# Attention values as the stationary operand, two key groups in column halves, and a division whose row sums travel through DRAM

## The chip, the cores and the metric

One core of a Trainium2 chip runs the whole program: two stacks of transformer blocks on 256 tokens of width 1024, in one launch, all in fp32. The metric is the device time of one execution in microseconds. TensorE multiplies, VectorE and ScalarE do the elementwise work, GpSimd (POOL) is nearly unused, and SP issues the DMAs.

## The reference

The first stack has two layers of feed-forward, mixer, feed-forward; so has the second, with another mixer. What the change touches is the attention in each mixer and the matmul that takes its output:

```python
def windowed_gqa(q, k, v, sink):                 # first stack: 8 heads, 2 key groups of 4 heads, head size 64
    scores = einsum('bnqhgd,bnkhd->bhgnqk', qb, kb) * (HEAD_DIM ** -0.5)
    scores = where(valid, scores, -1e30)
    probs = softmax(concatenate([scores, sink_logit], -1), -1)[..., :-1]
    out = einsum('bhgnqk,bnkhd->bnqhgd', probs, vb)
...
y_attn = windowed_gqa(q, k, v, attn_sink) @ w_br_attn
...
def swa_sink_attention(q, k, v, sinks, band_bias, band_mask):   # second stack: 16 heads, 2 key groups of 8 heads
    m = maximum(max(s, -1, keepdims=True), sink)
    e = exp(s - m)
    p = e / (sum(e, -1, keepdims=True) + exp(sink - m))
    o = einsum('bnkgqs,bnskd->bnqkgd', p, vb)
...
branch = einsum('blmc,mcd->blmd', ys, w_branch[l])    # ys[2] is the attention's output
```

## The kernel before, in words

A token block is 128 tokens (t = 0, 1) and lies on the 128 partitions. Every large matmul (`mm`, lines 346 to 361) takes its activations transposed, as pairs of a rounded part `ah` and a rest `al`, and its weights as pairs `whi` and `wlo`; three products L359, L360, L361 replace one exact fp32 product. A weight unit is two blocks of 128 rows by 512 columns: SP loads it into `raw` (`load_raw`, L253), ScalarE rounds it to `whi` (L268), VectorE takes the rest `wlo` (L274). For a unit TensorE does 12 products: two row blocks, two token blocks, three products each. The splits run several units ahead (`ahead`: 7 in the first mixer, 6 in the second), and up to four raw units wait besides.

The order of all engines is the order of the code. After each unit a `tick` (L319 on) issues the splits, then delayed pieces of work (`later`), then one step of the first task in a list. The attentions are such tasks: `attend1` (L639, first mixer) runs beside the gate projections, `attend2` (L852, second mixer) beside the three convolution projections and the gates of branch 2. In the first mixer the branch matmul that takes `yatt` follows right behind the task, in the second it is `branch(2, yatt, ...)`.

Both attentions go through `pipeline` (L700) in units u: a unit is a token block and four or eight heads. In iteration u it issues scores(u) and values(u - 2), then, one tick later, exps(u) and turn(u - 1).

- scores: fp32 products of head size 64 on half of the array's rows, even and odd heads in turn (L663, L875); VectorE adds the band or the bias and takes the row maxima (L580).
- exps: ScalarE's exponentials with row sums `den` (L588).
- turn: TensorE transposes the exponentials (L473), VectorE and ScalarE copy them to `pT` (L679, L681, L895, L897).
- values (L683, L899): for every head and key block a product with `pT` as the stationary operand, 128 by 128, and 64 columns of v moving (L690, L908). The output has queries on partitions. When eight heads are there, `inv_den` (L591) computes the reciprocals of the row sums, VectorE multiplies the PSUM tile by them, broadcast along the free axis (L695, L915), and in the next iteration `put_T` (L476) transposes the result with four TensorE transposes (L473) and splits it into `ah` and `al` (L485 on ScalarE, L487 on VectorE). These are the activations `yatt` of the branch matmul.

Small PSUM tiles come from four rotating buffers (`sm`), SBUF tiles of 2 KB per partition from twelve (`half`), and those of 4 KB from 41 (`big`).

Of the kernel before, what the change touches and what calls it, by code (L numbers as in the profile page):

```python
# [21 lines left out]
P = 128  # L22
# [111 lines left out]
def units(name, idx, segs, nkt):  # L134
    return [(name, idx, k, min(2, nkt - k), tuple(segs)) for k in range(0, nkt, 2)]
# [63 lines left out]
class Net:  # L199
# [53 lines left out]
    def load_raw(self):  # L253
        name, idx, k, m, segs = self.plan[self.raw_at]
# [221 lines left out]
    def put_T(self, act, kt0, t, src, m, scale=None, col=None, later=None):  # L476
# [6 lines left out]
        if col is None:  # L483
            o, l_ = hi[:, j0:j0 + m, ts], lo[:, j0:j0 + m, ts]
            nc.scalar.activation(o, ps[:, :m], AF.Copy, scale=1.0 if scale is None else scale)  # L485
            if scale is None:
                nc.vector.tensor_tensor(l_, ps[:, :m], o.bitcast(F32), ALU.subtract)  # L487
            else:
                nc.vector.scalar_tensor_tensor(l_, ps[:, :m], scale, o.bitcast(F32), ALU.mult, ALU.subtract)
        else:  # L490
            for j in range(m):
                nc.scalar.activation(hi[:, j0 + j, ts], ps[:, j], AF.Copy, scale=col(kt0 + j))  # L492
            for j in range(m):
# [3 lines left out]
                low() if later is None else later.append(low)  # L497

# [92 lines left out]
    def inv_den(self, den, mx, sink, n):  # L591

        nc = self.nc
        e = self.tiny([P, n])
# [3 lines left out]
        r = self.tiny([P, n])  # L598
        nc.vector.reciprocal(r, e)
        return r  # L600

# [37 lines left out]
    def attend1(self, l, qk, v, yatt):  # L639
# [11 lines left out]
        mx, den, po, sc, pT = {}, {}, {}, {}, {}  # L651
# [20 lines left out]

        def turn(u):
            s = sc.pop(u)
            p = pT[u] = self.big([P, 2, 4, P], s="pT")
            for kb in range(2):
                ps = self.transposed([s[:, h, kb * P:(kb + 1) * P] for h in range(4)])
                if kb:
                    nc.scalar.activation(p[:, kb], ps, AF.Copy)  # L679
                else:  # L680
                    nc.vector.tensor_copy(p[:, kb], ps)  # L681
# [16 lines left out]
        yield from self.pipeline(4, scores, exps, turn, values)  # L698

    def pipeline(self, n, scores, exps, turn, values):  # L700

        last = None
        for u in range(n + 2):
            if last is not None:
                last()
                last = None
            if u < n:
                scores(u)
            if u >= 2:
                last = values(u - 2)  # L710
# [6 lines left out]
        if last is not None:  # L717
            last()
# [25 lines left out]
    def mixer1(self, l, prep, nxt, after=None):  # L744
# [43 lines left out]
        for m, (gen, act, wb) in enumerate(((pool, ypool, "w_branch_pool"), (att, yatt, "w_branch_attn"))):  # L788
# [6 lines left out]
            for h in range(2):  # L795
                self.branch(act, units(wb, (l,), [(h * 512, 512, 0)], 4), th[h], y, h, m == 0)
# [55 lines left out]
    def attend2(self, l, qT, kd, va, yatt):  # L852
# [9 lines left out]
        plan = [(0, 0, 8), (0, 8, 8), (1, 0, 4), (1, 4, 4), (1, 8, 4), (1, 12, 4)]  # L862
        mx, den, po, sc, pT = {}, {}, {}, {}, {}
# [22 lines left out]

        def turn(u):
# [3 lines left out]
            blocks = [(e, kb) for e in range(per) for kb in range(t + 1)]  # L891
# [7 lines left out]
        def values(u):  # L899
            t, h0, per = plan[u]  # L900
            kv = h0 // 8
            if h0 % 8 == 0:
# [537 lines left out]
```

## Time and profile before

| | before |
|---|---|
| median of 3 runs | 2532.87 us (2532.43 to 2534.51) |
| the profiled execution | 2532.06 us |
| its span, first to last instruction | 2530.3 us |
| granted TensorE clock | 0.999 of 2.4 GHz |
| busy: TensorE, VectorE, ScalarE, GpSimd | 99%, 63%, 49%, 0% |

The sum in the prediction is made against the profiled execution; the runs stand some 0.8 us above it. In the rows, `sm<-v,pT` names the output tile and what it was computed from, PEld is a weight load, and a line number is a line of the kernel before. An fp32 product outside the large matmuls appears as two records.

### The profile page before, as it was taken

Reading aid. Unit: us, or ns where it says so; the run is one execution under the profiler, and the core shown is the slowest. Engines: PE = TensorE matmul, PEld = TensorE weight load, DVE = VectorE, ACT = ScalarE, POOL = GpSimd, SP = SyncE. Lnnn points to the kernel's source line nnn. Section 1 sums busy time; section 2 is a strip of 40 time slices with the busy share of each in tenths; the row PEclk is TensorE's granted clock in tenths of the full one; section 3 lists DMA queues with packets and bytes.
Section 4 is the critical chain, followed back from the end, with each engine's and each line's share of the span. In section 5 each row is a group of like instructions: output and inputs, shape, how many; then the busy total and the mean of one; then the engine's idle time right before and its main releaser. Section 6 shows DMA issues by size and latency. Waiting matters only on the chain.

```text
span 2530.3 us, 31764 instructions
## 1 busy us (share of the span) xinstructions
PE 2516.7 (99%) x12017; PEld 2083.6 (82%) x12017; DVE 1584.5 (63%) x2592; ACT 1239.3 (49%) x1882; POOL 0.2 (0%) x4
## 2 busy tenths in 40 slices
PE   9999999999999999999999999999999999999998
PEld 7888888888888888888888888888888888888887
DVE  6545665555546755655697777755654788776653
ACT  5435554444445544444474545543543664544542
POOL 0000000000000000000000000000000000000000
PEclk9999999999999999999999999999999999999999
DMA  8666555655564655655644566655656644566652
GB/s 285 212 203 211 158 191 166 201 188 174 178 218 149 199 167 186 200 178 187 207 125 142 175 192 196 199 175 194 197 168 199 184 130 146 185 194 206 185 179 79
DMA packets 252790, 462.26 MB, mean 183 GB/s; under 512 B 17707, under 2 KB 43996, under 8 KB 252508
## 3 DMA queue, kind: packets, MB, share of 16 engines
q1 hardware_dynamic: 252636, 460.23, 57.9%
q8 instruction: 94, 1.54, 0.2%
q14 instruction: 60, 0.49, 0.1%
HBM read 459.10 MB, written 4.22 MB: 183 GB/s over the span
## 4 chain that ended last, share of the span: by engine, by line
PE 95%; DVE 2%; ACT 2%; DMA 0%; issue 0%; SPq 0%; DVEq 0%; ACTq 0%
PE mm L359 29%; PE mm L361 29%; PE mm L360 29%; PE sm L473 4%; PE sm L908 1%; PE sm L690 1%; PE sm L1073 1%; DVE wlo L274 0%; ACT sc L588 0%; DVE acc L975 0%; PE sm L663 0%; ACT acc L968 0%; PE sm L1140 0%; ACT whi L268 0%; DVE sc L580 0%
## 5 line engine op out<-in xcount | busy, mean ns | idle before, releaser
L359 PE MATMUL mm<-whi,ah 128*128 128x512 f32 x3360 | 1326.2, 395 | 0.6 <-ACT whi L268 0.6
L361 PE MATMUL mm<-whi,al 128*128 128x512 f32 x3360 | 1304.5, 388 | 0.0
L360 PE MATMUL mm<-wlo,ah 128*128 128x512 f32 x3360 | 1301.9, 387 | 0.8 <-DVE wlo L274 0.8
L274 DVE TENSOR_TENSOR wlo<-raw,whi 128x1024 fp32r<-128x1024 f32 (+2 forms) x840 | 976.3, 1210 | 106.1 <-ACT whi L268 102.3
L268 ACT ACTIVATE whi<-raw 128x1024 fp32r<-128x1024 f32 (+2 forms) x840 | 829.2, 1048 | 104.8 <-PE mm L360 58.2
L361 PEld LDWEIGHTS mm<-whi,al 128*128 128x128 f32 x3360 | 630.7, 188 | 133.9 <-DVE al L495 4.1
L359 PEld LDWEIGHTS mm<-whi,ah 128*128 128x128 f32 x3360 | 631.3, 188 | 127.1 <-issue 4.3
L360 PEld LDWEIGHTS mm<-wlo,ah 128*128 128x128 f32 x3360 | 631.7, 188 | 126.3 <-issue 1.9
L485 ACT ACTIVATE ah<-sm 128x512 fp32r<-128x512 f32 (+1 forms) x124 | 64.7, 568 | 468.9 <-PE sm L473 465.5
L487 DVE TENSOR_TENSOR al<-sm,ah 128x512 fp32r<-128x512 f32 (+1 forms) x108 | 65.9, 647 | 170.7 <-ACT ah L485 170.7
L512 DVE SCALAR_TENSOR_TENSOR hid<-mm,s,silu 128x512 f32<-128x512 f32 (+1 forms) x96 | 66.9, 705 | 167.8 <-PE mm L361 153.8
L492 ACT ACTIVATE ah<-sm,cols 128x128 fp32r<-128x128 f32 x240 | 67.6, 374 | 146.8 <-PE sm L473 140.2
L495 DVE SCALAR_TENSOR_TENSOR al<-sm,cols,ah 128x128 fp32r<-128x128 f32 x240 | 68.1, 345 | 68.5 <-ACT ah L492 68.5
L507 ACT ACTIVATE silu<-mm,s 128x512 f32<-128x512 f32 (+1 forms) x96 | 62.0, 655 | 91.6 <-PE mm L361 90.7
L560 DVE SCALAR_TENSOR_TENSOR yg<-mm,post 128x512 f32<-128x512 f32 x24 | 16.6, 692 | 121.0 <-ACT sq L461 121.0
L544 DVE SCALAR_TENSOR_TENSOR x<-mm,x 128x512 f32<-128x512 f32 x24 | 16.5, 689 | 110.8 <-PE mm L361 110.8
L461 ACT ACTIVATE sq<-mm 128x512 bf16<-128x512 f32 x24 | 14.3, 597 | 125.8 <-PE mm L361 125.8
L613 ACT ACTIVATE gate<-gate 128x512 f32<-128x512 f32 x40 | 25.1, 632 | 52.1 <-DVE gate L612 51.7
L473 PEld LDWEIGHTS sm<-c_ident,hid 128*128 128x128 f32 x352 | 41.2, 140 | 6.8 <-DVE hid L512 0.7
L473 PE MATMUL sm<-c_ident,hid 128*128 128x128 f32 x352 | 46.5, 272 | 0.1
L588 ACT ACTIVATE sc<-sc,s 128x256 f32<-128x256 f32 (+1 forms) x96 | 43.9, 459 | 3.7 <-DVE s L583 3.6
L461 ACT ACTIVATE sq<-x 128x1024 bf16<-128x1024 f32 x26 | 27.4, 1069 | 22.6 <-DVE x L544 17.5
(200 smaller groups left out, 1022.0 us busy)
## 6 DMA issues: line engine op xcount, KB each, us to landing
raw<-in_ffn_w SPq DMA_DIRECT2D x248, 512.0 KB, 4.2
raw<-in_w_in SPq DMA_DIRECT2D x200, 512.0 KB, 3.7
raw<-in_w_ffn_in SPq DMA_DIRECT2D x160, 512.0 KB, 3.8
raw<-in_w_ffn_out SPq DMA_DIRECT2D x88, 512.0 KB, 3.9
raw<-in_w_branch SPq DMA_DIRECT2D x48, 512.0 KB, 3.5
raw<-in_w_out SPq DMA_DIRECT2D x32, 512.0 KB, 3.7
raw<-in_ffn_w SPq DMA_DIRECT2D x32, 256.0 KB, 3.0
raw<-in_w_ffn_in SPq DMA_DIRECT2D x32, 256.0 KB, 3.2
```

Source lines behind the costliest of these rows:

```text
L268: self.nc.scalar.activation(hi[:, :m, :width], raw[:, :m, :width], AF.Copy)
L274: self.nc.vector.tensor_tensor(lo[:, :m, :width], raw[:, :m, :width], hi[:, :m, :width].bitcast(F32), ALU.subtract)
L359: nc.tensor.matmul(ps[:, :n], a_h, hi[:, j, :n], start=(kt == 0), stop=False)
L360: nc.tensor.matmul(ps[:, :n], a_h, lo[:, j, :n], start=False, stop=False)
L361: nc.tensor.matmul(ps[:, :n], a_l, hi[:, j, :n], start=False, stop=(kt == nkt - 1))
L473: self.nc.tensor.transpose(ps[:, j, :], a, self.ident)
L485: nc.scalar.activation(o, ps[:, :m], AF.Copy, scale=1.0 if scale is None else scale)
L487: nc.vector.tensor_tensor(l_, ps[:, :m], o.bitcast(F32), ALU.subtract)
L492: nc.scalar.activation(hi[:, j0 + j, ts], ps[:, j], AF.Copy, scale=col(kt0 + j))
L495: nc.vector.scalar_tensor_tensor(lo[:, j0 + j, ts], ps[:, j], col(kt0 + j), hi[:, j0 + j, ts].bitcast(F32), ALU.mult, ALU.subtract)
L507: nc.scalar.activation(s[:, :n], ps, AF.Silu, scale=prep.rstd[t])
L512: nc.vector.scalar_tensor_tensor(h[:, :n], ps, prep.rstd[t], s[:, :n], ALU.mult, ALU.mult)
```

## The change

The roles in the value product are swapped. For a block of four heads e of each key group g, v of the group (128 keys by 64) is stationary and the transposed exponentials of the four heads (128 keys by 512) move. The group g writes to partitions 64g to 64g + 63 of one PSUM tile, in a column half of the array: group 0 in columns 0 to 63, group 1 in columns 64 to 127. The output is already transposed, channels on partitions, so the four transposes fall away. The reciprocal of a row sum now has to lie along the free axis and be the same on 64 partitions: POOL writes the reciprocals to a DRAM tile `rd` and reads them back, spread over 64 partitions for each group, to `rden`. `norm` does this one iteration after the scores; the multiply (`rest`) comes at the start of the iteration after the values. A unit's values need both groups: half of the units issue none, the others one block of four products (the first token block of `attend2` two blocks of two). `attend2` takes its units in another order for this.

The channels now lie in another order on the partitions: the first 64 hold heads of group 0, the others of group 1. The branch weights are loaded to match, each half of the partitions by a DMA of its own (`groups=2`).

```diff
-def units(name, idx, segs, nkt):
-    return [(name, idx, k, min(2, nkt - k), tuple(segs)) for k in range(0, nkt, 2)]
+def units(name, idx, segs, nkt, groups=1):
+
+    return [(name, idx, k, min(2, nkt - k), tuple(segs), groups) for k in range(0, nkt, 2)]
...
-            self.nc.sync.dma_start(raw[:, :m, at:at + n],
-                                   w[k * P:(k + m) * P, c0:c0 + n].rearrange("(k p) n -> p k n", p=P))
+            rows = w.shape[0] // groups
+            d = P // groups
+            for g in range(groups):
+                r = g * (rows if groups > 1 else 0)
+                self.nc.sync.dma_start(raw[g * d:(g + 1) * d, :m, at:at + n],
+                                       w[r + k * d:r + (k + m) * d, c0:c0 + n].rearrange("(k p) n -> p k n", p=d))
...
+    def spread(self, r, ne):
+
+        d = self.dp.tile([2, ne, P], F32, name=self.name("rd"))
+        self.nc.gpsimd.dma_start(d.rearrange("g e q -> q g e"), r)
+        out = []
+        for e in range(0, ne, 4):
+            R = self.half([P, 4, P], s="rden")
+            for g in range(2):
+                self.nc.gpsimd.dma_start(R[g * 64:g * 64 + 64].rearrange("p e q -> p (e q)"),
+                                         d[g, e:e + 4].rearrange("e q -> (e q)").partition_broadcast(64))
+            out.append(R)
+        return out
+
+    def weighted(self, v, pT, nkb, R, yatt, kt0, t):
+
+
+        nc = self.nc
+        ps = self.smp([P, 4, P])
+        for kb in range(nkb):
+            for g in range(2):
+                nc.tensor.matmul(ps[g * 64:g * 64 + 64].rearrange("p e q -> p (e q)"), v[kb][:, g * 64:g * 64 + 64],
+                                 pT[g][:, 4 * kb:4 * kb + 4].rearrange("p e q -> p (e q)"),
+                                 start=(kb == 0), stop=(kb == nkb - 1))
+
+        def rest():
+            o = self.half([P, 4, P], s="att")
+            nc.vector.tensor_tensor(o, ps, R, ALU.mult)
+            self.put(yatt, kt0, t, o, 4)
+        return rest
...
+        def norm(u):
+            t, half = divmod(u, 2)
+            if half == 1:
+                r[t] = self.spread(self.inv_den(den[t], mx[t], sink, 0, 4), 4)
...
         def values(u):
             t, half = divmod(u, 2)
-            if half == 0:
-                po[t] = self.smp([P, 8, 64])
-            p = pT.pop(u)
-            for e in range(4):
-                for kb in range(2):
-                    nc.tensor.matmul(po[t][:, half * 4 + e], p[:, kb, e], v[kb][:, half * 64:half * 64 + 64],
-                                     start=(kb == 0), stop=(kb == 1))
             if half == 1:
-                r = self.inv_den(den[t], mx[t], sink, 8)
-                o = self.half([P, 8, 64], s="att")
-                nc.vector.tensor_tensor(o, po[t], bcast(r, 2, 64), ALU.mult)
-                return lambda: self.put_T(yatt, 0, t, o.rearrange("p h d -> p (h d)"), 4)
+                return [self.weighted(v, [pT.pop(u - 1), pT.pop(u)], 2, r.pop(t)[0], yatt, 0, t)]
...
-        for u in range(n + 2):
-            if last is not None:
-                last()
-                last = None
+        for u in range(n + 3):
+            for f in rest or ():
+                f()
+            rest = ()
             if u < n:
                 scores(u)
-            if u >= 2:
-                last = values(u - 2)
+            if 1 <= u <= n:
+                norm(u - 1)
+            if 2 <= u < n + 2:
+                rest = values(u - 2)
+            if u == n + 2:
+                return
             yield
...
-        plan = [(0, 0, 8), (0, 8, 8), (1, 0, 4), (1, 4, 4), (1, 8, 4), (1, 12, 4)]
+        plan = [(0, 0, 8), (0, 8, 8), (1, 0, 4), (1, 8, 4), (1, 4, 4), (1, 12, 4)]
...
+            if h0 >= 8:
+                r[u] = self.spread(self.inv_den(den[t], mx[t], sinks, h0 - 8, per), per)
...
+            return [self.weighted(va, [q[:, e0:] for q in p] if t == 0 else p, t + 1, d[e0 // 4], yatt, h0 - 8 + e0, t)
+                    for e0 in range(0, per, 4)]
```

`put` is the second half of `put_T` without the transposes: ScalarE's rounding copy and VectorE's subtraction.

The change rewrites the order of several engines. Three places of it follow, as listings of the program, one line an instruction.

TensorE in the first attention, layer 0, before: the end of one weight unit, the transposes of the first token block's output (`att`), a block of eight value products, and the first product of the next unit.

```order
L361 MATMUL mm_2337<-whi_2216,al_1607 128x512
L473 MATMUL sm_2472<-c_ident,att_2417 128x128 x4
L690 MATMUL sm_2479<-v_1853,pT_2441 128x64
L690 MATMUL sm_2479<-v_1864,pT_2441 128x64
L690 MATMUL sm_2479<-v_1853,pT_2441 128x64
L690 MATMUL sm_2479<-v_1864,pT_2441 128x64
L690 MATMUL sm_2479<-v_1853,pT_2441 128x64
L690 MATMUL sm_2479<-v_1864,pT_2441 128x64
L690 MATMUL sm_2479<-v_1853,pT_2441 128x64
L690 MATMUL sm_2479<-v_1864,pT_2441 128x64
L359 MATMUL mm_2496<-whi_2238,ah_1604 128x512
```

The same engine in the change, at the last value block of this attention, between two weight units:

```order
L366 MATMUL mm_2491<-whi_2273,al_1605 128x512
L636 MATMUL sm_2541<-pT_2436,v_1853 64x512
L636 MATMUL sm_2541<-pT_2510,v_1853 64x512
L636 MATMUL sm_2541<-pT_2436,v_1864 64x512
L636 MATMUL sm_2541<-pT_2510,v_1864 64x512
L364 MATMUL mm_2490<-whi_2309,ah_1606 128x512
```

Two key groups (`pT_2436`, `pT_2510`) alternate, 64 output partitions each; four products stand where 16 of 64 columns stood in two blocks, and no transposes follow.

VectorE in the second attention, layer 0, before: the reciprocals of the row sums of eight heads, the multiply of the PSUM tile, the next weight split.

```order
L595 TENSOR_TENSOR s_10841<-rows,s_10514 128x8
L597 TENSOR_TENSOR s_10841<-s_10841,s_10515 128x8
L599 RECIPROCAL s_10845<-s_10841 128x8
L915 TENSOR_TENSOR att_10847<-sm_10832,s_10845 128x512
L274 TENSOR_TENSOR wlo_10861<-raw_10644,whi_10805 128x1024
```

In the change the chain ends with the reciprocals of all sixteen heads of token block 0, and a weight split follows at once, with no multiply behind it:

```order
L596 TENSOR_SCALAR s_10657<-s_10657 128x4
L609 TENSOR_TENSOR s_10671<-rows,s_10474 128x16
L611 TENSOR_TENSOR s_10671<-s_10671,s_10475 128x16
L613 RECIPROCAL s_10675<-s_10671 128x16
L279 TENSOR_TENSOR wlo_10705<-raw_10518,whi_10651 128x1024
L1025 SCALAR_TENSOR_TENSOR acc_10501<-th_10653,acc_10501 128x512
```

Thirty rows later comes the multiply, between a weight split and the row maxima of the next scores; it takes the spread tile `rden`:

```order
L279 TENSOR_TENSOR wlo_10841<-raw_10649,whi_10804 128x1024
L642 TENSOR_TENSOR att_10852<-sm_10782,rden_10679 128x512
L508 TENSOR_TENSOR al_10346<-att_10852,ah_10345 128x4x128
L642 TENSOR_TENSOR att_10856<-sm_10785,rden_10682 128x512
L508 TENSOR_TENSOR al_10348<-att_10856,ah_10347 128x4x128
L593 ISA sc_10860,s_10657<-sm_10861,T_9997,rows 128x256
```

POOL in the change, where the first stack's last attention ends and the second's begins: the write of the reciprocals `s` of eight heads to DRAM, element by element, and two reads back; then the write of sixteen heads and four reads; then eight again. Before, POOL has no DMA at all.

```order
L619 DMA rd_6610<-s_6608 128x8x1
L624 DMA rden_6612<-rd_6610 64x512 x2
L619 DMA rd_10677<-s_10675 128x16x1
L624 DMA rden_10679<-rd_10677 64x512 x2
L624 DMA rden_10682<-rd_10677 64x512 x2
L619 DMA rd_10878<-s_10876 128x8x1
```

Each write is followed at once by its reads, which can start only when it has landed. The program has ten writes and 24 reads.

## Rows read from the trace of the kernel before

**Rows 1.** The page's first part: busy time, share and instructions of each engine.

```profile
PE 2516.7 (99%) x12017; PEld 2083.6 (82%) x12017; DVE 1584.5 (63%) x2592; ACT 1239.3 (49%) x1882; POOL 0.2 (0%) x4
```

**Rows 2.** The page's chain that ended last, by engine.

```profile
PE 95%; DVE 2%; ACT 2%; DMA 0%; issue 0%; SPq 0%; DVEq 0%; ACTq 0%
```

**Rows 3.** Groups of TensorE by line and shape: xcount | busy us, mean ns.

```profile
L908 PE MATMUL sm<-va,pT 128*128 128x64 f32 x192 | 23.6, 276 | 1.0 <-DVE pT L897 0.5 <-ACT pT L895 0.4
...
L690 PE MATMUL sm<-v,pT 128*128 128x64 f32 x128 | 15.6, 275 | 0.0
...
L473 PE MATMUL sm<-c_ident,att 128*128 128x128 f32 x48 | 7.2, 271 | 0.0
```

**Rows 4.** Timeline of TensorE, 300 to 322 us: start us, us, engine, line, names.

```profile
303.56 0.39 PE L359 MATMUL mm<-whi,ah 128*128 128x512 f32 x1
...
304.25 0.60 PE L473 MATMUL sm<-c_ident,att 128*128 128x128 f32 x4
...
305.38 0.40 PE L359 MATMUL mm<-whi,ah 128*128 128x512 f32 x1
```

**Rows 5.** Timeline of TensorE, 284 to 300 us.

```profile
296.29 0.39 PE L359 MATMUL mm<-whi,ah 128*128 128x512 f32 x1
...
296.97 1.89 PE L690 MATMUL sm<-v,pT 128*128 128x64 f32 x16
298.67 0.48 PE L359 MATMUL mm<-whi,ah 128*128 128x512 f32 x1
...
299.45 0.40 PE L359 MATMUL mm<-whi,ah 128*128 128x512 f32 x1
```

**Rows 6.** Timeline of all engines, 1361.5 to 1365 us (PEld: weight load).

```profile
1362.00 0.39 PE L359 MATMUL mm<-whi,ah 128*128 128x512 f32 x1
1362.01 0.19 PEld L360 LDWEIGHTS mm<-wlo,ah 128*128 128x128 f32 x1
...
1362.23 0.39 PE L360 MATMUL mm<-wlo,ah 128*128 128x512 f32 x1
...
1362.68 1.02 PE L1060 MATMUL sm<-st,acc 128*128 128x512 f32 x2
...
1363.14 0.80 PE L359 MATMUL mm<-whi,ah 128*128 128x512 f32 x1
...
1364.25 0.39 PE L359 MATMUL mm<-whi,ah 128*128 128x512 f32 x1
```

**Rows 7.** Timeline of TensorE, 244 to 262 us.

```profile
254.49 0.39 PE L359 MATMUL mm<-whi,ah 128*128 128x512 f32 x1
...
255.27 1.14 PE L663 MATMUL sm<-kT,qT 64*128 64x256 f32 x8
256.33 0.50 PE L359 MATMUL mm<-whi,ah 128*128 128x512 f32 x1
...
257.13 0.40 PE L359 MATMUL mm<-whi,ah 128*128 128x512 f32 x1
```

**Rows 8.** Timeline of TensorE, 255.26 to 255.30 us.

```profile
255.27 0.49 PE L663 MATMUL sm<-kT,qT 64*128 64x256 f32 x2
```

**Rows 9.** Timeline of all engines, 268 to 300 us.

```profile
269.62 1.13 PE L663 MATMUL sm<-kT,qT 64*128 64x256 f32 x8
...
279.04 1.13 PE L663 MATMUL sm<-kT,qT 64*128 64x256 f32 x8
...
282.66 0.20 DVE L599 RECIPROCAL s<-s 128x8 f32<-128x8 f32 x1
```

**Rows 10.** DMA issues by line: xcount, KB each, median us to landing.

```profile
T<-fb SPq DMA_DIRECT2D x32, 128.0 KB, 2.7
...
bias<-in_b_gate SPq DMA_DIRECT2D x20, 256.0 KB, 4.7
...
raw<-in_w_in SPq DMA_DIRECT2D x8, 16.0 KB, 3.5
```

**Rows 11.** Windows view, 1288 to 1320 us: length; busy PE, PEld, DVE, ACT, POOL; clock, DMA.

```profile
1288.00:1320.00 32.00, 31.50 (x197) 26.20 (x195) 29.25 (x70) 24.91 (x57) 0.00 (x0) 1.00 0.37 117
```

More of the change, by code (lines that the diff above doesn't have):

```diff
@@ L253, in load_raw @@
     def load_raw(self):
-        name, idx, k, m, segs = self.plan[self.raw_at]
+        name, idx, k, m, segs, groups = self.plan[self.raw_at]
         self.raw_at += 1
@@ L483, in put_T @@
         if col is None:
[L484 to L489, printed above, removed]
+            self.put(act, kt0, t, ps, m, scale)
         else:
@@ L589, in row_exp, with inv_den @@
                                       accum_out=den[:, h0 + h:h0 + h + 1])
-    def inv_den(self, den, mx, sink, n):
+    def inv_den(self, den, mx, sink, e0, ne):
         nc = self.nc
-        e = self.tiny([P, n])
+        den, mx, sink = (v.rearrange("p (g e) -> p g e", g=2)[:, :, e0:e0 + ne] for v in (den, mx, sink))
+        e = self.tiny([P, 2, ne])
         nc.vector.tensor_tensor(e, sink, mx, ALU.add)
@@ L650, in attend1 @@
         sink = self.rows[:, l, 0:8]
-        mx, den, po, sc, pT = {}, {}, {}, {}, {}
+        mx, den, sc, pT, r = {}, {}, {}, {}, {}
         def scores(u):
@@ L716, in pipeline @@
             yield
-        if last is not None:
-            last()
     def pool1(self, l, pt, ypool):
@@ L795, in mixer1 @@
             for h in range(2):
-                self.branch(act, units(wb, (l,), [(h * 512, 512, 0)], 4), th[h], y, h, m == 0)
+                self.branch(act, units(wb, (l,), [(h * 512, 512, 0)], 4, 1 + m), th[h], y, h, m == 0)
                 if m:
@@ L885, in exps, with norm @@
             self.row_exp(sc[u], per, mx[t], den[t], h0)
+        def norm(u):
+            t, h0, per = plan[u]
+            if h0 >= 8:
+                r[u] = self.spread(self.inv_den(den[t], mx[t], sinks, h0 - 8, per), per)
         def turn(u):
@@ L890, in turn @@
             p = pT[u] = self.big([P, 8, P], s="pT")
-            blocks = [(e, kb) for e in range(per) for kb in range(t + 1)]
+            blocks = [(e, kb) for kb in range(t + 1) for e in range(per)]
             for b in range(2):
@@ L900, in values @@
             t, h0, per = plan[u]
-            kv = h0 // 8
-            if h0 % 8 == 0:
-                po[t, kv] = self.smp([P, 8, 64])
-            p = pT.pop(u)
-            i = 0
-            for e in range(per):
-                for kb in range(t + 1):
-                    nc.tensor.matmul(po[t, kv][:, (h0 + e) % 8], p[:, i], va[kb][:, kv * 64:kv * 64 + 64],
-                                     start=(kb == 0), stop=(kb == t))
-                    i += 1
-            if (h0 + per) % 8 == 0:
-                hs = slice(8 * kv, 8 * kv + 8)
-                r = self.inv_den(den[t][:, hs], mx[t][:, hs], sinks[:, hs], 8)
-                o = self.half([P, 8, 64], s="att")
-                nc.vector.tensor_tensor(o, po[t, kv], bcast(r, 2, 64), ALU.mult)
-                return lambda: self.put_T(yatt, 4 * kv, t, o.rearrange("p h d -> p (h d)"), 4)
-        yield from self.pipeline(6, scores, exps, turn, values)
+            if h0 < 8:
+                return ()
+            p = [pT.pop(u - 1), pT.pop(u)]
+            d = r.pop(u)
+            return [self.weighted(va, [q[:, e0:] for q in p] if t == 0 else p, t + 1, d[e0 // 4], yatt, h0 - 8 + e0, t)
+                    for e0 in range(0, per, 4)]
+        yield from self.pipeline(6, scores, exps, norm, turn, values)
     def decays(self, l, dtr, out):
@@ L1223, in branch @@
             for h in range(2):
-                self.branch(act, units("w_branch_2", (l, m), [(h * 512, 512, 0)], 8), th[h], y, h, first, scale)
+                self.branch(act, units("w_branch_2", (l, m), [(h * 512, 512, 0)], 8, 2 if m == 2 else 1), th[h], y, h, first,
+                            scale)
                 if then is not None:
```

27 lines of the change are left out of this document (19 added, 8 removed).

## The prediction, made before the changed kernel was run

> **What bounds the kernel now.** I read the page first: TensorE is busy for 2516.7 of 2530.3 us, VectorE for 63% of the span, ScalarE for 49%, GpSimd for nothing [rows 1]. A busy share alone can deceive, since matmuls are pipelined, so the second view is the chain of work that ended last: 95% of it is TensorE, 2% each VectorE and ScalarE, and the queues of SP, VectorE and ScalarE have 0% [rows 2]. So the span is the sum of what TensorE has to do, and an instruction taken off it shortens the program by its time, as long as nobody becomes late. The third view is the groups by line, with shapes apart: the value products of the two attentions are 192 and 128 records of 64 columns, and the turning of the attention output is 48 transposes [rows 3]. Each fp32 product is two records, so that is 96 and 64 products. The fourth view is TensorE's timeline, where I price each kind of block by what it delays.
>
> **How a block is priced.** In steady state three weight products (L359, L360, L361) take 0.68 us: L359 starts at 296.29 and the next thing at 296.97 [rows 5]. A block's price is how much later the second L359 behind it starts than it would have without the block. The second, because the first one after a block of small products starts slowly.
>
> **What goes.** A block of eight value products: it starts at 296.97; without it the L359 rows would be at 296.97 and 297.65, and the second one is at 299.45 [rows 5]. Price 1.80 us. There are 160 products, 20 blocks: 36.0 us. Four transposes of the attention output: they start at 304.25, the second L359 should be at 304.93 and is at 305.38 [rows 4]. Price 0.45 us, and 12 such blocks: 5.4 us. Together **41.4 us leave TensorE**.
>
> **What comes.** 40 products of 512 columns with 64 stationary columns each, in 10 blocks of four: two blocks a layer in attend1, three in attend2 (its first query block issues two pairs one behind the other, which also makes four products). No row of before shows a product on half of the columns. The nearest for its length is the carried state of the scan, one fp32 product of 512 columns on the whole array: L359 at 1362.00, so the second L359 behind is due at 1363.36 and stands at 1364.25 [rows 6]. Price 0.89 us. The nearest for running side by side are the score products of attend1: four products of 256 columns, each on half of the rows, alternating between the halves. By the row above a product of 256 columns costs half of 0.89, and four in turn would be 1.78 us. The block starts where an L359 was due at 255.17; the second L359 should be at 255.85 and is at 257.13, so the block costs 1.28 us [rows 7]. And a window of 0.04 us at its start holds two matmuls already begun [rows 8]. So two halves do run beside each other: two pairs at 0.445 are 0.89 us, and 0.39 us is left for entering and leaving the half-array form.
>
> The upper bound of a new block is all four in turn, 4 x 0.89 + 0.39 = 3.95 us, ten of them 39.5. The lower bound is pairs side by side, 2 x 0.89 + 0.39 = 2.17 us, ten of them 21.7. I take the lower, since the scores are the same kernel, the same type and the same order of issue (one half, the other half), and differ only in that the halves are rows instead of columns. TensorE then saves 41.4 - 21.7 = **19.7 us**.
>
> Against it speaks how weights are loaded: two row halves share no row, two column halves share all. In the full-array stream the load for L360 starts at 1362.01, with L359 at 1362.00 still in flight, and is over before L360 begins at 1362.23 [rows 6], so a load under a running product on the same rows costs nothing here. The Trainium skill (TensorE: Matmul & The Clock Gate, Part 3: Packing small matmuls) says that a weight load overlaps with products in flight only when their row groups differ. The row contradicts it for the whole array; whether it holds for column halves no row of before shows. By that rule the pairs would not run together.
>
> **The division.** The multiply by the reciprocal stays one VectorE instruction per block of heads, and so do the copy and the subtraction that split the output (12 of each before and after). They read an SBUF tile instead of PSUM for the split: nothing. Twelve reciprocal chains become ten. What is new is the way of the reciprocals: POOL writes them to DRAM element by element, waits for that, reads them back twice, 64 partitions each, and VectorE's multiply waits for both reads. Behind that multiply on VectorE stand the next row maxima and splits; for it wait the PSUM tile of the product and, on TensorE, whoever gets that tile next, or the branch product.
>
> The cover: norm of a unit comes one iteration after its scores, the multiply two iterations after that. An iteration takes 279.04 - 269.62 = 9.42 us, and the reciprocal begins 3.62 us into its own and lasts 0.20 [rows 9]. Two iterations are 18.8, less 1.8 for the value block that the first of them loses, plus 0.4 for the longer block in the second, less 3.8: **13.6 us of cover**. TensorE itself has more: the transposes that would get the tile, or the branch's first use of that half, come behind one or more units of twelve products, 2.7 us, and what is queued with it, so some 4 us more.
>
> The price of the trip: no DMA of before is issued by POOL and none has pieces of 4 bytes. The nearest are 16 KB in 256 pieces (two runs of 16 numbers per partition), 3.5 us, 128 KB in 128 pieces (one run per partition), 2.7 us, and a row spread over 128 partitions, 4.7 us [rows 10]. If pieces cost nothing, write and read are 3.5 + 4.7 = 8.2 us. If they cost what lies between 128 and 256 pieces, 0.8 us per 128, 1024 pieces (8 heads) need 2.7 + 7 x 0.8 = 8.3, with the read 13.0 us; 2048 pieces (16 heads, once per layer in attend2) need 14.7, with the read 19.4 us. Against 13.6 us that is on time for 8 heads, and 6 us late for VectorE, 2 us for TensorE, on the two trips of 16 heads: 4 us. I take the middle of 0 and 4, **2 us**. The Trainium skill (DMA: Bandwidth & Descriptors, Rules for kernel authors) says that a non-contiguous last dimension becomes one descriptor per element; by it the write is the dear kind, and the deduction would be the 4, with 2517 as the sum.
>
> The loads of the branch weights become two DMAs of half the partitions, 24 more on SP, whose queue has no part in the chain [rows 2]; they are asked for several units ahead. If SP were late, the splits would be, and after them TensorE; I see no sign. In the stretch of attend2 VectorE is busy for 29.25 of 32 us [rows 11]; TensorE gives back 6 x 1.80 + 4 x 0.45 - 3 x 2.17 = 6.1 us per layer over the whole of attend2, so VectorE stays just under it.
>
> **Sum.** 2532.06 (the profiled execution, 2530.3 span and 1.8 around it) - 19.7 + 2.0 = 2514.4. The median of the runs stands 0.8 above the profiled one, so I forecast **2515 us**, 0.7% faster.
>
> **The rivals.** A measurement of this kernel can tell 0.2% (5 us) from no change, and the limits are 2527.8 and 2537.9.
>
> (A) The column halves take turns. For it: all rows are shared, and no row shows them together. Against: the row halves, which do. Price: 39.5 instead of 21.7, so 41.4 - 39.5 = 1.9 us of gain, **2531 us**: no change. If weight loads stood in the open as well, it would be a little slower than that.
>
> (B) The reciprocals come late. The multiply stands on VectorE, and with it TensorE. It decides from about 17.6 us per trip, and it makes the kernel slower than before from 25 us lost in ten trips, 2.5 each, so from a trip of about 20 us. The dear end of the rows: if 256 pieces need 3.5 us and pieces were all of it, 1024 need 14 and 2048 need 28, with the read 18.7 and 32.7 us; eight trips lose 1 us and two 15 us each, 38 us: 2515 - 2 + 38 = **2551 us**. For it: POOL has no DMA here that could show its speed. Against: 256 pieces of 64 bytes need hardly more than 128 of 1024 bytes, so most of a DMA's time is not its pieces.
>
> (C) VectorE becomes the bound in attend2. At 29.25 of 32 us it has 9% to spare, and the new multiply waits for PSUM and then ScalarE for it. If each of TensorE's savings there (6 us a layer) were lost, the gain is 19.7 - 12 = 8 us, **2525 us**: still faster.
>
> That the change doesn't do what it says is no case of weight: TensorE's order holds the four 512-column products and no transposes.
>
> **Chances.** Forecast 0.62; A 0.14 (0.10 within the limit, 0.04 slower, with loads in the open); B 0.12 (0.03 faster, 0.03 within, 0.06 slower); C 0.12, faster. So faster 0.62 + 0.03 + 0.12 = 0.77, same 0.10 + 0.03 = 0.13, slower 0.10. The forecast's own range is 2510 to 2520: below, no late trip (2 us) and the 0.39 us of entering shared by the six blocks that stand right behind scores (2.3 us); above, up to 5 us of further waits. To hold 8 in 10 it has to reach over C to A: 2510 to 2531.
>
> **What would show it.** Right: the groups of 64-column products are gone; ten blocks of 512-column, 64-wide products whose two halves start within some 0.01 us of each other; the second L359 behind such a block 2.2 us late; the multiply's wait for the DMA near zero; POOL's reads landing under 13 us after the reciprocal. Wrong: halves that start 0.4 us or more apart in one file, or a wait of VectorE for rden of several us with an idle TensorE behind it.

## The result and the profile of the changed kernel

The changed kernel takes **2573.3 us** (median, 2572.0 to 2575.2), the kernel before 2532.7 us: a ratio of 1.0163, interval 1.015 to 1.0175. It is 40.6 us slower; the forecast was 2515 us, faster.

First the page of the changed kernel: busy time, and the chain that ended last by engine.

```profile
span 2570.2 us, 31318 instructions
...
PE 2516.3 (98%) x11729; PEld 2056.0 (80%) x11729; DVE 1583.0 (62%) x2586; ACT 1238.4 (48%) x1880; POOL 22.6 (1%) x38
...
PE 42%; DVE 1%; DMA 1%; ACT 1%; issue 0%; DVEq 0%; POOL 0%; ACTq 0%; POOLq 0%
```

Against [rows 1] TensorE has 288 instructions fewer and is busy for just as long (2516.3 against 2516.7 us); its idle time, span less busy, went from 13.6 to 53.9 us. The chain could be followed back over 45% of the span only, where it covered the span, 95% of it on TensorE, in [rows 2]. So two things happened: TensorE waits, and the instructions that are left take longer. The waits of the changed kernel (us in total, times, longest us) tell for what:

```profile
DVE att L642 <- DMA rden<-rd: 70.1, 10, 10.2
...
PE sm L478 <- ACT xbc L995: 13.5, 4, 6.2
PE sm L636 <- DVE pT L943: 10.2, 2, 5.6
PE mm L364 <- ACT ah L506: 8.0, 2, 4.6
PE sm L636 <- DVE pT L730: 7.8, 2, 4.1
```

VectorE's multiply waits for the spread reciprocals in all ten trips, 7 us each on average. In TensorE's list no DMA of the trip stands: it waits for copies and splits of VectorE and ScalarE that stand behind that multiply (6.8 of the 13.5 us for xbc stay without the trip, see below). The windows view over the four attentions (busy by engine, then TensorE's clock) says where:

```profile
220.00:330.00 110.00, 101.68 (x476) 78.57 (x475) 67.50 (x123) 52.02 (x92) 4.04 (x6) 0.95 0.59 170
780.00:880.00 100.00, 92.55 (x423) 70.66 (x423) 59.71 (x111) 46.23 (x89) 3.94 (x6) 0.95 0.55 158
1300.00:1450.00 150.00, 136.73 (x667) 105.49 (x666) 114.30 (x218) 77.72 (x144) 7.19 (x11) 0.97 0.53 137
2050.00:2190.00 140.00, 128.11 (x621) 98.01 (x620) 108.98 (x223) 74.54 (x146) 7.22 (x11) 0.95 0.54 132
```

Here TensorE idles 41 of 500 us, and the granted clock is 0.95 to 0.97. Now two trips one after the other, in the first attention. GpSimd's timeline (in brackets: idle before, and what ended it by the profile):

```profile
273.27 1.03 POOL L619 DMA_DIRECT2D rd<-s  x1 [272.83 <-DVE s L613]
284.16 1.04 POOL L624 DMA_DIRECT2D rden<-rd  x2 [9.86 <-PE sm L478]
294.60 0.93 POOL L619 DMA_DIRECT2D rd<-s  x1 [9.40 <-DVE s L613]
304.56 1.04 POOL L624 DMA_DIRECT2D rden<-rd  x2 [9.04 <-DMA rd<-s]
```

VectorE's in the same stretch:

```profile
272.76 0.20 DVE L613 RECIPROCAL s<-s 128x8 f32<-128x8 f32 x1
...
283.82 1.22 DVE L279 TENSOR_TENSOR wlo<-raw,whi 128x1024 fp32r<-128x1024 f32 x1
291.47 0.69 DVE L642 TENSOR_TENSOR att<-sm,rden 128x512 f32<-128x512 f32 x1 [6.44 <-DMA rden<-rd]
...
294.11 0.20 DVE L613 RECIPROCAL s<-s 128x8 f32<-128x8 f32 x1
...
311.23 0.69 DVE L642 TENSOR_TENSOR att<-sm,rden 128x512 f32<-128x512 f32 x1 [10.19 <-DMA rden<-rd]
```

The reciprocals are done at 272.96, the write is issued, the reads follow 10.9 us later (the bracket names a transpose of TensorE, but without the write the reads don't wait, as a run below shows), and the multiply starts at 291.47: **18.5 us**. VectorE was free at 285.04, so the cover was 12.1 us. The next reciprocals stand behind that late multiply, at 294.11 to 294.31; VectorE was free for the second multiply at 301.04, so that trip has only 6.7 us of cover, takes 16.9 and makes VectorE wait 10.2. Lateness is handed on to the next trip. And TensorE:

```profile
292.64 1.07 PE L636 MATMUL sm<-pT,v 128*64 128x512 f32 x2
297.39 3.59 PE L636 MATMUL sm<-pT,v 128*64 128x512 f32 x6 [3.68 <-DVE pT L730]
...
307.61 0.39 PE L366 MATMUL mm<-whi,al 128*128 128x512 f32 x1
312.63 0.80 PE L364 MATMUL mm<-whi,ah 128*128 128x512 f32 x1 [4.63 <-ACT ah L506]
313.23 0.63 PE L365 MATMUL mm<-wlo,ah 128*128 128x512 f32 x1
313.65 0.63 PE L366 MATMUL mm<-whi,al 128*128 128x512 f32 x1
...
317.49 0.55 PE L366 MATMUL mm<-whi,al 128*128 128x512 f32 x1
317.88 0.39 PE L364 MATMUL mm<-whi,ah 128*128 128x512 f32 x1
```

It waits for pT, a copy that stands behind the multiply on VectorE, then for the branch matmul's `ah`. Behind the second wait its products follow each other every 0.43 us, from 313.23 to 317.49, and every 0.23 us from 317.88 on. The granted clock from 312.60 to 317.50 is 0.50: 1.2 instead of 2.4 GHz, after an idle stretch of 4.63 us. TensorE has eight stalls of over 3 us in the four attentions, 3.4 to 6.2 us long, and behind each of them products run for 3.0 to 5.4 us at a granted clock of 0.50. These stalls are paid for twice.

The column halves do what was forecast:

```profile
276.46 0.39 PE L366 MATMUL mm<-whi,al 128*128 128x512 f32 x1
276.78 1.14 PE L707 MATMUL sm<-kT,qT 64*128 64x256 f32 x8
277.84 1.94 PE L636 MATMUL sm<-pT,v 128*64 128x512 f32 x8
279.71 0.50 PE L364 MATMUL mm<-whi,ah 128*128 128x512 f32 x1
...
280.51 0.39 PE L364 MATMUL mm<-whi,ah 128*128 128x512 f32 x1
```

Without scores and values the L364 rows would stand at 276.69 and 277.37; the second is at 280.51, 3.14 us late. 1.28 of that are the scores [rows 7], so the block costs 1.86 us. It stands right behind the scores, where the forecast, 2.17 us, gave 1.78 (without the 0.39 us of entering); a block that stands alone costs 2.09 us in the run without a trip (start 292.58, second L364 at 295.27). A window of 0.04 us at its start, 277.83 to 277.87, holds two of its matmuls:

```profile
277.84 0.65 PE L636 MATMUL sm<-pT,v 128*64 128x512 f32 x2
```

They are not the two records of one product: where group 1's first product had to wait for pT, the two records of group 0's ran one behind the other, 1.07 us (292.64 above). So a product on half of the columns is not shorter by itself; two of them run side by side.

### The profile page after: what moved, and what is told of

Its sections match the earlier page's. It is cut to its first block, busy times and chain, and to the rows that moved or that the text cites. A ratio compares the mean times of both kernels' runs of the same rounds, so it can differ in the third digit from the quotient of the medians.

```text
span 2570.2 us, 31318 instructions
## 1 busy us (share of the span) xinstructions
PE 2516.3 (98%) x11729; PEld 2056.0 (80%) x11729; DVE 1583.0 (62%) x2586; ACT 1238.4 (48%) x1880; POOL 22.6 (1%) x38
## 3 DMA queue, kind: packets, MB, share of 16 engines
q0 software_dynamic: 1504, 3.20, 0.5%
## 5 line engine op out<-in xcount | busy, mean ns | idle before, releaser
L364 PE MATMUL mm<-whi,ah 128*128 128x512 f32 x3360 | 1328.6, 395 | 8.0 <-ACT ah L506 8.0
L364 PEld LDWEIGHTS mm<-whi,ah 128*128 128x128 f32 x3360 | 633.1, 188 | 148.5 <-issue 17.2
L506 ACT ACTIVATE ah<-sm 128x512 fp32r<-128x512 f32 (+1 forms) x112 | 57.6, 565 | 441.4 <-PE sm L478 438.1
L508 DVE TENSOR_TENSOR al<-sm,ah 128x512 fp32r<-128x512 f32 (+1 forms) x96 | 57.6, 642 | 149.2 <-ACT ah L506 149.2
L642 DVE TENSOR_TENSOR att<-sm,rden 128x512 f32<-128x512 f32 x12 | 8.3, 691 | 70.1 <-DMA rden<-rd 70.1
L506 ACT ACTIVATE ah<-att 128x512 fp32r<-128x512 f32 x12 | 7.6, 630 | 81.7 <-DVE att L642 81.7
```

The source lines that it names most:

```text
L364: nc.tensor.matmul(ps[:, :n], a_h, hi[:, j, :n], start=(kt == 0), stop=False)
```

## The experiments

The theory: the trip by way of DRAM is late, and all of the loss is TensorE's waiting and the lower clock behind it. Rivals: the new products, or the new order, cost the time; the DMAs disturb others; one piece of the trip is the dear one. All ratios are against the kernel before, run on the same chip. The medians of its runs beside the experiments lie within 0.3 us of each other, so the times of the experiments are compared with each other too.

**No trip.**

```diff
     def spread(self, r, ne):
+        return [None] * (ne // 4)
...
-            nc.vector.tensor_tensor(o, ps, R, ALU.mult)
+            nc.vector.tensor_tensor(o, ps, bcast(self.ones, 1, 4), ALU.mult)
```

> The trip by way of DRAM is left out; the product is multiplied by a resident tile of ones, so the division is left out, all else stands. Theory (the trip is late; everything TensorE lost is waiting and a lower clock after it): no wait of the multiply, granted clock back to 0.998 or more, 2532 - 41.4 + 18.7 = about 2510 us, 2507 to 2516. Rival (the products on column halves, or the order in which the groups alternate, cost TensorE the time): it stays above 2550 us. Half and half would be near 2540 us.

2520.0 us, ratio 0.9953 (0.9938 to 0.9967), granted clock 0.998: 53 us faster than the changed kernel, but above the 2507 to 2516 that were expected. Its page:

```profile
PE 2498.8 (99%) x11729; PEld 2049.4 (81%) x11729; DVE 1583.5 (63%) x2586; ACT 1239.5 (49%) x1880; POOL 0.2 (0%) x4
```

The span is 2517.5. Taking the trip away gives 52.7 us of span: 35.2 of TensorE's idle time (53.9 to 18.7) and 17.5 of busy time in the same 11729 instructions, at a mean clock of 0.990 against 0.998. The eight stretches at half clock fit that: products run in them for 32.2 us, and half of it, 16.1 us, is an estimate of what they cost. The trip is the cause; but 2520 is not 2510, and what lies between has another cause (below).

**The trip, and nobody waits.** Only the second edit above: the DMAs are issued.

> As the run without a trip, but GpSimd issues all ten writes and 24 reads, and nobody waits for them; the multiply takes the tile of ones, so the division is left out. Theory (only the wait costs): within 3 us of the run without a trip. Rival (the DMAs themselves disturb: they delay the weight loads, or GpSimd's issue holds VectorE): at least 10 us above the run without a trip, with wlo and raw among what TensorE waits for.

2525.4 us, ratio 0.9974 (0.9964 to 0.9983), its nine runs 2521.7 to 2528.8: 5.4 us more than without a trip, between the two expectations. The waits view, of the slowest of the nine, says who is held up:

```profile
ACT whi L273 <- DMA raw<-in_w_branch: 24.8, 4, 12.8
```

and the DMA issues (KB each, median us to landing) by what:

```profile
raw<-in_w_branch SPq DMA_DIRECT2D x32, 256.0 KB, 13.7
```

Without the trip the same half loads of the branch weights land in 4.1 us. So DMAs on different queues do get in each other's way, though the wait is by far the larger part: 47.9 us of the 53.3.

**The reads alone.** The write is left out; the reads fetch from a DRAM tile of ones.

```diff
-        d = self.dp.tile([2, ne, P], F32, name=self.name("rd"))
-        self.nc.gpsimd.dma_start(d.rearrange("g e q -> q g e"), r)
+        d = self.rdc[:, :ne]
+        self.nc.gpsimd.tensor_copy(self.tiny([P, 2, ne]), r)
...
```

> The write is left out: the 24 reads fetch from a DRAM tile that holds ones since the start, so the division is left out; GpSimd copies the reciprocals first, so the reads are issued after the reciprocals as before. Theory (the write with its landing is 10 to 14.6 us of each trip, the reads 3 to 9 us): the reads land 5 to 10 us after the reciprocals, within the 12.1 us of cover, so the multiply hardly waits and the time is that of the run without a trip, within 5 us. Rival (the spreading reads, 64 times each row, are the dear part): above 2535 us.

2521.1 us, ratio 0.9957 (0.994 to 0.9973): as without a trip, and the multiply never waits for a DMA. Spreading to 64 partitions is not the dear part. The branch weights land in 5.1 us here, so it is not the reads that slow them.

**The write in dense pieces.**

```diff
-        self.nc.gpsimd.dma_start(d.rearrange("g e q -> q g e"), r)
+        self.nc.gpsimd.dma_start(d.rearrange("g e q -> (g e q)").rearrange("(q n) -> q n", q=P),
+                                 r.rearrange("q g e -> q (g e)"))
```

> The write goes to DRAM in the order of SBUF, 128 pieces of 32 bytes (64 for sixteen heads) instead of 1024 or 2048 pieces of 4 bytes; issue, bytes, reads and waits stand (the reads then spread the numbers in another order, so the division uses wrong rows). Theory (a fixed 7 us and 3.5 us per 1024 pieces): the write lands in 7 to 8 us instead of 10.6 and 13.2, each trip 3 to 6 us shorter, the multiply's wait falls from 70 to about 25 us, and the time to about 2535 us, 2525 to 2550. If the pieces are nearly all of it: write under 4 us and 2510 to 2516 us. If pieces cost nothing: 2573 us.

2521.2 us, ratio 0.9956 (0.994 to 0.9973), nearly the run without a trip, and above the 2510 to 2516 expected for this case, as that run is. Its DMA issues:

```profile
raw<-in_w_branch SPq DMA_DIRECT2D x32, 256.0 KB, 5.6
...
rd<-s POOLq DMA_DIRECT2D x8, 4.0 KB, 3.3
...
rd<-s POOLq DMA_DIRECT2D x2, 8.0 KB, 1.7
```

and in the changed kernel, with GpSimd's queue (packets, MB, share of the DMA engines) first:

```profile
q0 software_dynamic: 1504, 3.20, 0.5%
...
raw<-in_w_branch SPq DMA_DIRECT2D x32, 256.0 KB, 10.2
...
rd<-s POOLq DMA_DIRECT2D x8, 4.0 KB, 10.6
...
rd<-s POOLq DMA_DIRECT2D x2, 8.0 KB, 13.2
```

The same 4 KB land in 3.3 instead of 10.6 us, 8 KB in 1.7 instead of 13.2, and the branch weights come sooner too. My "fixed 7 us" fell with this run: what looked fixed were pieces.

**The same write from ScalarE's queue.**

```diff
-        self.nc.gpsimd.dma_start(d.rearrange("g e q -> q g e"), r)
+        self.nc.scalar.dma_start(d.rearrange("g e q -> q g e"), r)
```

> The same write of 4-byte pieces, issued from ScalarE's queue instead of GpSimd's; the reads stay with GpSimd. If GpSimd's way of making the pieces is the dear part, the write lands in 3 to 5 us, and the time falls to 2510 to 2525 us. If the pieces themselves or the landing are, it still lands in some 10 us, and the time stays at 2560 to 2580 us. ScalarE's own wait for the reciprocals is 1 us at most, ten times.

2575.1 us, ratio 1.017 (1.0155 to 1.0185): no better. Its queues (packets, MB) and issues:

```profile
q0 software_dynamic: 1152, 3.15, 0.5%
q10 hardware_dynamic: 12448, 0.05, 0.2%
...
rd<-s ACTq DMA_DIRECT2D x8, 4.0 KB, 10.7
...
rd<-s ACTq DMA_DIRECT2D x2, 8.0 KB, 11.8
```

Some 12,000 packets for 0.05 MB on ScalarE's queue: eight writes of 1024 and two of 2048 numbers make 12,288, a packet a number. On GpSimd's queue the count of packets doesn't show the pieces: 1504 with the writes in the changed kernel, 1152 for the reads alone here, so some 350 for the ten writes. But from GpSimd the dense write lands early and the one of 4-byte pieces late, and from ScalarE that one is as late: it is the pieces, not GpSimd.

**More cover.** `norm` moves one tick ahead, behind the exponentials.

```diff
-            if 1 <= u <= n:
-                norm(u - 1)
...
             if 1 <= u <= n:
                 turn(u - 1)
+            if u < n:
+                norm(u)
```

> The whole computation is kept; only the reciprocals and the trip start one tick earlier, right behind the exponentials, some 4.7 us more cover. Theory (lateness against the cover, passed on from one trip to the next): the multiply's wait falls from 70 us to about 20, the clock rises, time 2520 to 2542 us. If the trip is not what counts: 2573 us. A new wait: VectorE stands until ScalarE's exponentials are done, some 2 us, ten times, which TensorE need not feel.

2542.5 us, ratio 1.004 (1.0025 to 1.0055): 31 us better than the changed kernel, just above what was expected. The multiply still waits 43.3 us, in six trips of ten, where about 20 were expected. Cover helps; there isn't enough of it.

**No trip, the division kept: scaling the exponentials.** Before the transposes queries lie on partitions, so the reciprocals need no spreading.

```diff
+        nc.gpsimd.tensor_tensor(s, s, bcast(r, 2, s.shape[2]), ALU.mult)
...
-            nc.vector.tensor_tensor(o, ps, R, ALU.mult)
-            self.put(yatt, kt0, t, o, 4)
+            self.put(yatt, kt0, t, ps, 4)
```

> The whole computation is kept, without a trip: GpSimd multiplies the exponentials by the reciprocals while the queries still lie on partitions, before the transposes; the products stay transposed and go from PSUM straight into the split. Twenty multiplies of 1024 columns on GpSimd. Theory (column halves save 22 us, only the trip cost): 2505 to 2515 us if one such multiply takes under 4 us, since it starts about that long before the transposes. Rival (GpSimd is slow or holds VectorE): above 2525 us, with waits of the transposes L478 for GpSimd.

2553.7 us, ratio 1.0083 (1.0068 to 1.0098): the rival's case. And with VectorE in GpSimd's place:

> As the run with GpSimd's multiply, but VectorE does it: twenty multiplies of 1024 columns at about 1.2 us (a weight split of that size takes 1.21) come to VectorE, twelve of 0.69 us go, net 16 us. Theory: attend2 has VectorE at 29 of 32 us, so it becomes the bound there for some us: 2512 to 2525 us. If VectorE has room: as the run with GpSimd, or better.

2535.8 us, ratio 1.0015 (1.0005 to 1.0024): better by 18 us, but above the 2512 to 2525 expected. GpSimd's multiply takes 2.33 us, as its group shows:

```profile
L626 POOL TENSOR_TENSOR sc<-sc,s 128x1024 f32<-128x1024 f32 x20 | 46.6, 2331 | 2046.1 <-DVE s L625 1996.0 <-ACT xbc L1002 32.8 <-DMA bias<-in_b_gate 9.4
```

and TensorE's transposes wait for it each time (waits view):

```profile
PE sm L478 <- POOL sc L626: 31.1, 20, 3.5
```

VectorE's (1.22 us) still holds the transposes for 15.9 us, twelve times. Neither is a way out: the division then stands on TensorE's path, where in the changed kernel it has two iterations.

**The halves in turn.** No trip, and each block does both products of group 0, then both of group 1.

```diff
-        for kb in range(nkb):
-            for g in range(2):
+        for g in range(2):
+            for kb in range(nkb):
```

> No trip (the division is left out), and in each block of four products first both of group 0, then both of group 1, instead of in turn. If the alternation is what lets the column halves run side by side, a block of two key blocks costs up to 2 x 0.89 us more, eight such blocks up to 14 us: 2530 to 2535 us. If the halves run beside each other in any order, or never did: within 2 us of the run without a trip, 2518 to 2522 us.

2519.8 us, ratio 0.9953 (0.9936 to 0.9969): no difference, and the start of a block, a window of 0.04 us, again holds two:

```profile
277.58 0.66 PE L637 MATMUL sm<-pT,v 128*64 128x512 f32 x2
```

The order of issue isn't what lets the halves run together. By the reading above these two belong to two products as well; then group 1's first began ahead of group 0's second, though the trace's names don't tell which they are.

**The ten microseconds left.** In the run without a trip the first mixer's attentions gain what the blocks say, and the second's don't. TensorE's timeline there:

```profile
1301.56 0.39 PE L366 MATMUL mm<-whi,al 128*128 128x512 f32 x1
1304.30 1.47 PE L478 MATMUL sm<-c_ident,xbc 128*128 128x128 f32 x8 [2.35 <-ACT xbc L996]
```

and ScalarE's:

```profile
1303.46 0.21 ACT L610 ACTIVATE s<-s 128x8 f32<-128x8 f32 x1 [2.65 <-DVE s L609]
1303.57 1.25 ACT L996 ACTIVATE xbc<-mm,s 128x512 f32<-128x512 f32 x2
```

The small exponential of the sinks waits for VectorE, and the copies that TensorE needs stand behind it. The edit issues it with the row exponentials, half an iteration earlier:

```diff
-        nc.scalar.activation(e, e, AF.Exp)
...
+            if half == 1:
+                es[u][1]()
             self.row_exp(sc[u], 4, mx[t], den[t], half * 4)
```

> What is open: without the trip the time is 2520 us, not 2510. The run without a trip gains 4.15 us in each of the first mixer's attentions, as the blocks say, but only 1.4 and 2.5 us in the second mixer's, where the blocks say about 7. There TensorE waits 2.4 us for the copies xbc of ScalarE, which stand behind the small exponential of the sinks; that one waits for VectorE's row maxima. Edit: no trip (the division is left out), and the exponential of the sinks moves to ScalarE's place of the row exponentials, half an iteration earlier, so that nothing of it stands ahead of the copies. Theory (that wait is what is lost): the waits for xbc vanish and the time falls by 4 to 8 us, to 2512 to 2516 us. Rival (VectorE's own load is the bound there, whoever stands first): within 2 us of 2520.

2516.6 us, ratio 0.9941 (0.9927 to 0.9956): 3.4 us of the ten, just short of what was expected, and TensorE's waits for xbc fall from 6.8 to 1.3 us.

Then VectorE's own wait: in `rest` it stands 0.70 us for ScalarE's rounding copy, twelve times. The edit moves the subtraction behind the next row maxima:

```diff
-            for f in rest or ():
-                f()
+            lows = [f() for f in rest or ()]
             rest = ()
             if u < n:
                 scores(u)
+            for f in lows:
+                f()
```

> The same without a trip (the division is left out): what the swapped product gives when the spread costs nothing. If VectorE's 0.7 us waits are the rest of what the second mixer lost: 2510 to 2514 us, with TensorE waiting less for the copy pT than the 1.4 us, twice, of the run with the earlier sinks alone. If not: 2515 to 2518 us.

2513.9 us, ratio 0.9927 (0.9914 to 0.9941), as expected. Its page:

```profile
PE 2496.0 (99%) x11729; PEld 2047.4 (82%) x11729; DVE 1582.8 (63%) x2586; ACT 1238.7 (49%) x1880; POOL 0.2 (0%) x4
```

TensorE is busy for 20.7 us less than before; the forecast said 19.7. By the intervals neither edit by itself can be told from none, and even those of the first and the last of these three kernels overlap, by 0.0003. That the two edits together gain 6 us rests on the single runs, which lie apart (2519.3 to 2520.7 against 2512.9 to 2514.7).

**A version that keeps the division.** VectorE turns the reciprocals in blocks of 32 by 32 first, so the write has 128 pieces of 128 bytes:

```diff
+        self.nc.vector.transpose(self.rT[i], self.rp[i])
+        d = self.dp.tile([32, 4, 32], F32, name=self.name("rd"))
+        self.nc.gpsimd.dma_start(d.rearrange("j b i -> b j i"), self.rT[i])
+        d = d[:2 * ne].rearrange("(g e) b i -> g e (b i)", g=2)
```

> The whole computation is kept. VectorE turns the reciprocals in blocks of 32 by 32 before the write, so that the write has 128 pieces of 128 bytes instead of 1024 or 2048 of 4; the reads stand as they are. Theory (the 4-byte pieces are what made the trip late): the write lands in 2 to 4 us, and the time is that of the dense write, 2517 to 2524 us: faster than before by 0.4%. If the 16 KB or VectorE's extra instruction cost something of note: above 2526 us.

2522.5 us, ratio 0.9962 (0.9947 to 0.9976). With the sinks' exponential moved as well:

> The whole computation is kept: the turned write together with the earlier exponential of the sinks. If both act alone as expected, 2513 to 2519 us, the fastest of all kernels that keep the division. If the earlier exponential gains nothing: as the turned write alone.

2520.6 us, ratio 0.9956 (0.9941 to 0.9971): not the 2513 to 2519 expected. And with the subtraction moved too:

> The whole computation is kept: the turned write and the earlier exponential of the sinks, and VectorE's subtraction for al, which waits 0.7 us for ScalarE's rounding copy between two multiplies, moves behind the row maxima of the next scores. If VectorE's waiting there is what holds the second mixer's attention back: 2514 to 2519 us. If VectorE's work is the bound, not its waits: within 1.5 us of the kernel without this edit, 2520.6.

**2519.9 us**, ratio 0.995 (0.9937 to 0.9964): it beats both kernels, by 0.5% and 2.1%. The last two edits can't be told from none here: the intervals of the three overlap. What remains, 6 us above the same kernel without a trip, shows in part in its waits, though the write now lands in 3.7 us:

```profile
PE sm L643 <- DVE pT L960: 6.8, 2, 3.5
```

In the kernel without a trip this wait is 2.3 us. The copy pT stands behind a multiply that still waits, four times, 7.8 us in all. In the second mixer the reads of the eight-head trips follow the write's issue after 5.8 to 8.8 us, in the first after 2.6 to 4.4, so there the write itself is late again; which DMA makes it late was not tried.

## Why the prediction was wrong

**What leaves, and what comes, was right.** TensorE was busy for 17.9 us less than before in the run without a trip and for 20.7 less in the last one; 19.7 were forecast. The block costs 1.86 us behind scores and 2.09 alone; 1.78 and 2.17 were forecast. Rival A (halves take turns) is excluded by the two products begun within 0.04 us. The Trainium skill (TensorE: Matmul & The Clock Gate, Part 3: Packing small matmuls) has the rule, weighed ahead, that a weight load overlaps with products in flight only when row groups differ; the trace differs: two halves that share all rows run together, at 1.86 to 2.09 us a block against 3.56 to 3.95 in turn.

**The step that failed is the trip, "8.2 to 13.0 us" for eight heads, "on time".** From the reciprocals to the multiply it took 16.1 to 22.0 us. The 18.5 us of the rows above are 0.3 to the write's issue, 10.9 from there to the reads, and 7.3 for the reads and their issue. The upper end of the forecast had 8.3 for the write and 4.7 for the read, with nothing for issuing, which takes 0.9 to 1.2 us for a write and 0.5 for each read. So of the 5.5 us over 13.0 some 2.9 are the write's, 2.6 the reads'. The price of a piece is 1.7 us of that: 5.6 of the 8.3 us stood for pieces, at 0.8 us per 128 from two rows of whole runs [rows 10], neither of which has a piece under 64 bytes, and pieces of 4 bytes cost 10.6 - 3.3 = 7.3 us per write of 1024, as the dense write shows. The rest are the issues and the reads. For sixteen heads the same price gave 19.4 us, more than the 17.2 and 18.2 measured. What fell with it is the argument against rival B, that most of a DMA's time is not its pieces: here 7.3 of 10.6 us are. The Trainium skill (DMA: Bandwidth & Descriptors, Rules for kernel authors) says that a non-contiguous last dimension lowers to one descriptor per element; on ScalarE's queue the trace agrees, with 12,448 packets for ten writes, and on GpSimd's the packets don't show it. The prediction had this warning, with 2517 us by it, and left the forecast at 2515.

**The cover, "13.6 us", was one number for all trips.** The first has 12.1 us, the second 6.7: a late multiply stands ahead of the next reciprocals on VectorE. Averaging lateness over ten trips has no meaning when a trip starts from the last one's delay. TensorE did have some more cover, as forecast: waits of 6.44 and 10.19 us on VectorE left it idle for 3.68 and 4.63. But the first of these was for pT, a copy behind the multiply that the forecast did not name among those who wait.

**A late TensorE was priced at its wait alone.** 17.5 of the 52.7 us are longer products, which goes with the slower clock behind the waits; no term stood for it.

**Rival B was what happened**, with its mechanism as described and two sizes wrong: it blamed the sixteen-head trips, where all ten are late and the sixteen-head ones least (3.77 and 2.71 us), and it gave 2551 us, without the clock. Its chance of 0.12 looks small in view of the prediction's own rows: the range of prices reached 19.4 us, over the cover, and no row showed the operation.

**Rival C happened in small.** It priced 12 us for the second mixer; the run without a trip lacks 10 there and then gets 6 of them back by two edits that only move waits of ScalarE and VectorE. So more than half of it was not VectorE's load but who stands in front of whom. Of the other 4 us TensorE's waits for pT, 2.3 us in the last run, are a part; the rest stays open.

## What to carry to other kernels

Count the pieces of a DMA before its bytes: where the innermost run is one number, turn the data on chip first; here that was worth 51 us of 2573. When an edit puts a DMA's latency behind a queue, work out the cover for the second trip as if the first had been late, and add a slower clock to a long stall of TensorE: here it followed all eight of over 3 us, and one of two of 2.3 us in the run without a trip. Experiments that leave one piece of a new path out (wait, write, read, queue) tell which piece is the dear one.

## What was unexpected of the hardware

- Two products on column halves run beside each other in whatever order they are issued: 2519.8 us with groups in turn, 2520.0 us alternating.
- A write of 4 KB in 4-byte pieces slows weight loads on another queue: the 256 KB halves of the second mixer's branch weights landed in 13.7 us (median) with it, 5.1 with the reads alone, 4.1 without a trip.
- The queue makes little difference to such a write: 10.6 us from GpSimd and 10.7 from ScalarE for 1024 pieces, 13.2 and 11.8 for 2048.
- After 4.63 us of idleness TensorE went on at a granted clock of 0.50, 1.2 GHz, for twelve products, 0.43 us apart instead of 0.23.
